# 1080 products with unread results behind the last needed one, in 60 patterns of operand addresses and widths

## The chip, the cores and the metric

The kernel runs on one core of a Trainium2 chip, as one launch. The core has a matrix engine (TensorE, PE in the profile, with its weight loads shown apart as PEld), three engines for elementwise work (VectorE or DVE, ScalarE or ACT, GpSimd or POOL), and SyncE (SP), which here only issues DMAs. TensorE multiplies a stationary operand of up to 128 x 128 numbers, which a weight load puts into the array, with a moving operand of up to 512 columns, and writes into PSUM, a memory of eight banks. The operands lie in SBUF, the on-chip memory of 128 partitions.

The metric is the device time of the launch in microseconds (us), lower is better.

## The reference

A two-layer encoder trunk over 256 frames and 16 learned meta tokens, width 2048. Layer 0 has gated linear attention (four heads) and stick-breaking attention (eight heads) behind one input projection and one output projection; layer 1 is a Mamba-2 mixer with eight groups. Each layer ends in a residual sum and a layer norm. In shortened form:

```python
h = concat([pad, meta, x], axis=1)
f = even_mixer(h, valid, ev_w_in, ..., ev_w_out)
h = layer_norm(ALPHA * h + f, ln_g[0], ln_b[0])
f = odd_mixer(h, valid, od_w_in, ..., od_w_out)
h = layer_norm(ALPHA * h + f, ln_g[1], ln_b[1])
return h[:, PREFIX:]
```

All arrays are float32. The output is 256 x 2048.

## The kernel before

The weights come from memory in units of 128 x 2048 numbers (1 MB each), one DMA per unit on SP's queue into the tile `raw`. Each half unit is split into a high part `whi` and a low part `wlo` (`split_into`, L144 to L146: ACT copies with rounding, DVE or POOL subtracts), both of type float32r, in which a product takes one pass of the array. The activations are split in the same manner into `xhi` and `xlo`, each of 16 blocks of 288 columns, of which a product reads up to 274. A full product is then three float32r products: high by high, high by low, low by high (`three`, L163 to L165). Two of the three use the same stationary tile `whi`, and the weight load stands ahead of each of them all the same.

An input unit (`in_unit`) is 16 blocks times three products, 48 in a row, into one PSUM tile `pj`. Its moving operand has 272 columns, or 260 where the unit is "C" (it starts at column 12 of a block) or 256 where it is "z" (it starts at column 16). A block starts 288 columns behind the one before. An output unit of layer 1 (`out1_half`, L421 to L423) turns it round: the activations `yh`, `yl` are stationary and 512 columns of the weights move. Between such rows of products stand the small products of the mixers, as steps of generators that `tick` takes in turn.

The order on each engine is fixed when the program is built, by a scheduler that goes by the recorded order and priorities. Each engine runs its own list, and semaphores join the lists.

The end of the program is `tail` (L1098 on). It splits the last four weight units; two of these go into `xhi` and `xlo`, which are free by then and seen there as flat rows (of 4608 columns; 4096 are written). Then come the last output products of two token halves of 128 rows each (the second half's last 512 columns in two pieces of 256), the sums into `acc` (L430), the statistics (L1133, L1137), the layer norm (L1139 to L1152) and five output DMAs (L1153, L1154). PSUM tiles named `po` come from two banks, those named `pj` from four. At the very end SP waits for all the output DMAs and for the last count of each engine, and then all engines meet twice (L1206 in the profile).

Of the kernel before, what the change touches and what calls it, by code (L numbers as in the profile page):

```python
# [12 lines left out]
P = 128  # L13
# [53 lines left out]
NU = len(L0) + len(L1)  # L67
# [20 lines left out]
class _Body:  # L88
# [1009 lines left out]
    def tail(self):  # L1098

        nc, lp = self.nc, self.lp  # L1100
        vec, pool = nc.vector, nc.gpsimd
        i0, g = NU - 4, NG - 1
        self.drain()
        self.load_unit(i0 + 2)
        for n, dq in enumerate((1, 2)):
            for h in range(2):
                src = self.raw[i0 + dq][:, h * 1024 : (h + 1) * 1024]
                o = slice((2 * n + h) * 1024, (2 * n + h + 1) * 1024)
                hi, lo = [a.rearrange("p k t -> p (k t)")[:, o] for a in (self.xhi, self.xlo)]
                nc.scalar.activation(hi, src, AF.Copy)  # L1110
                vec.tensor_tensor(lo, src, hi.bitcast(F32), op=ALU.subtract)
                self.parts[i0 + dq, h] = (hi, lo)
            if n == 0:
                self.load_unit(i0 + 3)
        lg = self.hp.tile([P, D], F32, tag="hacc", name="lg")
        lb = lp.tile([P, D], F32, tag="M", name="lb")
        nc.sync.dma_start(lg, self.lnr_d[0].partition_broadcast(P))
        nc.sync.dma_start(lb, self.lnr_d[1].partition_broadcast(P))
        for h in range(2):
            self.split_half(i0 + 3, h)  # L1120
        for t in range(2):
            st = lp.tile([P, 8, 6], F32, tag="fst", name=self.nm("fst"), bufs=2)
            acc = self.acc[:, t, :]
            for dq in range(4):
                halves = (0, 1) if t == 1 and dq == 3 else (None,)
                for b in halves:
                    ps = self.pj()
                    for h in range(2):
                        self.out1_half(ps, g, t, *self.parts[i0 + dq, h], h, b)
                    self.out1_add(ps, g, t, dq, b)  # L1130
                    with self.tc.high_priority():
                        for c in range(2) if b is None else (b,):
                            vec.bn_stats(st[:, 2 * dq + c, :], acc[:, dq * 512 + c * 256 : dq * 512 + (c + 1) * 256])  # L1133
            mv = lp.tile([P, 2], F32, tag="fmv", name=self.nm("fmv"), bufs=2)
            v, r, tm, mr = [lp.tile([P, 1], F32, tag=f"f{n}", name=self.nm("f"), bufs=2) for n in range(4)]
            with self.tc.high_priority():
                vec.bn_aggr(mv, st)  # L1137
                vec.tensor_scalar(v, mv[:, 1:2], LN_EPS, None, op0=ALU.add)
                nc.scalar.activation(r, v, AF.Ln)  # L1139
                nc.scalar.activation(r, r, AF.Exp, scale=-0.5)  # L1140
                self.newton(r, v, tm)
                vec.scalar_tensor_tensor(mr, mv[:, 0:1], -1.0, r, op0=ALU.mult, op1=ALU.mult)
            cut = (0, 1024, 2048) if t == 0 else (0, 384, 1216, 2048)
            ch = [slice(a, b) for a, b in zip(cut, cut[1:])]
            for cs in ch[1:]:
                vec.scalar_tensor_tensor(acc[:, cs], acc[:, cs], mv[:, 0:1], lg[:, cs], op0=ALU.subtract, op1=ALU.mult)  # L1146
            a = acc[:, ch[0]]
            nc.scalar.activation(a, a, AF.Identity, bias=mr, scale=r)  # L1148
            pool.tensor_tensor(a, a, lg[:, ch[0]], op=ALU.mult)  # L1149
            pool.tensor_tensor(a, a, lb[:, ch[0]], op=ALU.add)  # L1150
            for cs in ch[1:]:
                vec.scalar_tensor_tensor(acc[:, cs], acc[:, cs], r, lb[:, cs], op0=ALU.mult, op1=ALU.add)  # L1152
                nc.sync.dma_start(self.out[t * P : (t + 1) * P, cs], acc[:, cs])  # L1153
            nc.sync.dma_start(self.out[t * P : (t + 1) * P, ch[0]], a)  # L1154


def _pack(i):
# [53 lines left out]
```

## Time and profile before

| what | value |
|---|---|
| time, median of 2 runs | 1452.59 us (1452.31 to 1452.87) |
| the profiled execution's own time | 1453.08 us |
| its span, from the first to the last instruction | 1451.4 us |
| what lies outside of the span | 1453.08 - 1451.4 = 1.68 us |
| TensorE products in the profile | 10780 records |
| granted TensorE clock, mean | 0.996 |

A product's record is longer than the distance to the next one: products overlap in the array, so a record of 0.29 us stands every 0.126 us. What one more product costs is therefore not its record's length but the distance from one start to the next, and that is read from the first and the last row of a stretch without gaps and the number of products in it. A float32 product that isn't float32r takes two passes and leaves two records.

### The profile page before, as it was taken

Reading aid. Unit: us, or ns where it says so; the run is one execution under the profiler, and the core shown is the slowest. Engines: PE = TensorE matmul, PEld = TensorE weight load, DVE = VectorE, ACT = ScalarE, POOL = GpSimd, SP = SyncE. Lnnn points to the kernel's source line nnn. Section 1 sums busy time; section 2 is a strip of 40 time slices with the busy share of each in tenths; the row PEclk is TensorE's granted clock in tenths of the full one; section 3 lists DMA queues with packets and bytes.
Section 4 is the critical chain, followed back from the end, with each engine's and each line's share of the span. In section 5 each row is a group of like instructions: output and inputs, shape, how many; then the busy total and the mean of one; then the engine's idle time right before and its main releaser. Section 6 shows DMA issues by size and latency. Waiting matters only on the chain. (4 is left out here: it accounts for less than half of the span.)

```text
span 1451.4 us, 26046 instructions
## 1 busy us (share of the span) xinstructions
PE 1435.8 (99%) x10780; PEld 1360.0 (94%) x10780; DVE 985.9 (68%) x1516; ACT 761.9 (52%) x1125; POOL 346.3 (24%) x297
## 2 busy tenths in 40 slices
PE   9999999999999999999999999999999999999996
PEld 7999999999999999999999999899898998989975
DVE  8646575574564455446899979576876767768577
ACT  5535454454345444445577756555555555555541
POOL 4000000000101010112601435342432433434322
PEclk9999999999999999999999999999999999999998
DMA  7544444445444445434445554564554555444551
GB/s 259 203 163 161 158 156 157 170 146 175 147 173 149 142 145 175 164 141 146 145 146 213 193 205 164 203 222 169 198 175 167 199 180 215 153 171 171 203 204 58
DMA packets 36566, 249.82 MB, mean 172 GB/s; under 512 B 4128, under 2 KB 4960, under 8 KB 7776
## 3 DMA queue, kind: packets, MB, share of 16 engines
q1 hardware_dynamic: 36304, 247.90, 48.6%
q8 instruction: 84, 1.38, 0.4%
q14 instruction: 34, 0.28, 0.1%
q10 hardware_dynamic: 144, 0.26, 0.1%
HBM read 245.94 MB, written 2.20 MB: 171 GB/s over the span
## 5 line engine op out<-in xcount | busy, mean ns | idle before, releaser
L163 PE MATMUL pj<-xhi,whi 128*128 128x272 f32 (+4 forms) x2560 | 739.5, 289 | 1.9 <-ACT whi L145 1.6
L165 PE MATMUL pj<-xhi,wlo 128*128 128x272 f32 (+4 forms) x2560 | 737.7, 288 | 0.0
L164 PE MATMUL pj<-xlo,whi 128*128 128x272 f32 (+4 forms) x2560 | 734.6, 287 | 0.0
L146 DVE TENSOR_TENSOR wlo<-raw,whi 128x1024 fp32r<-128x1024 f32 (+1 forms) x402 | 512.0, 1276 | 293.2 <-ACT whi L145 292.1
L145 ACT ACTIVATE whi<-raw 128x1024 fp32r<-128x1024 f32 (+1 forms) x432 | 452.6, 1049 | 422.1 <-PE pj L164 349.7
L163 PEld LDWEIGHTS pj<-xhi,whi 128*128 128x128 f32 x2560 | 481.4, 188 | 5.7 <-ACT whi L145 2.3
L164 PEld LDWEIGHTS pj<-xlo,whi 128*128 128x128 f32 x2560 | 482.2, 188 | 1.7 <-DVE xlo L292 0.4
L165 PEld LDWEIGHTS pj<-xhi,wlo 128*128 128x128 f32 x2560 | 481.3, 188 | 2.3 <-DVE xlo L292 1.3
L163 PE MATMUL pj<-mixh,whi 128*128 128x272 f32 x384 | 112.4, 294 | 0.0
L164 PE MATMUL pj<-mixl,whi 128*128 128x272 f32 x384 | 111.1, 290 | 0.0
L165 PE MATMUL pj<-mixh,wlo 128*128 128x272 f32 x384 | 111.0, 289 | 0.0
L146 POOL TENSOR_TENSOR wlo<-raw,whi 128x1024 fp32r<-128x1024 f32 x30 | 73.8, 2461 | 140.7 <-ACT whi L145 140.7
L421 PE MATMUL pj<-whi,yh 128*128 128x512 f32 (+1 forms) x244 | 98.2, 402 | 0.0
L423 PE MATMUL pj<-whi,yl 128*128 128x512 f32 (+1 forms) x244 | 96.0, 393 | 0.0
L422 PE MATMUL pj<-wlo,yh 128*128 128x512 f32 (+1 forms) x244 | 95.6, 392 | 0.0
L252 POOL TENSOR_TENSOR gr<-gr,gsc 128x1088 f32<-128x1088 f32 x6 | 15.4, 2575 | 295.8 <-ACT gsc L251 295.8
L164 PEld LDWEIGHTS pj<-mixl,whi 128*128 128x128 f32 x384 | 72.3, 188 | 0.3
L163 PEld LDWEIGHTS pj<-mixh,whi 128*128 128x128 f32 x384 | 72.1, 188 | 0.5
L165 PEld LDWEIGHTS pj<-mixh,wlo 128*128 128x128 f32 x384 | 72.3, 188 | 0.1
L430 DVE SCALAR_TENSOR_TENSOR acc<-pj,rr,acc 128x512 f32<-128x512 f32 (+1 forms) x65 | 47.4, 737 | 30.3 <-PE pj L423 30.3
L1072 POOL TENSOR_TENSOR yu<-yu,gz 128x256 f32<-128x256 f32 x32 | 41.7, 1310 | 89.6 <-DVE yu L1071 89.4
L423 PEld LDWEIGHTS pj<-whi,yl 128*128 128x128 f32 x244 | 46.0, 188 | 10.6
(304 smaller groups left out, 1520.2 us busy)
## 6 DMA issues: line engine op xcount, KB each, us to landing
raw<-in_wts SPq DMA_DIRECT2D x214, 1024.0 KB, 4.8
ebc<-edr SPq DMA_DIRECT2D x8, 1664.0 KB, 6.7
hacc<-in_xT SPq DMA_DIRECT2D x8, 272.0 KB, 6.3
raw<-in_wts SPq DMA_DIRECT2D x8, 256.0 KB, 5.3
lg<-in_lnr SPq DMA_DIRECT2D x1, 1024.0 KB, 4.8
lb<-in_lnr SPq DMA_DIRECT2D x1, 1024.0 KB, 6.1
out_h<-acc SPq DMA_DIRECT2D x2, 512.0 KB, 2.6
out_h<-acc SPq DMA_DIRECT2D x2, 416.0 KB, 2.5
```

The costliest lines, as they stand in the source:

```text
L145: self.nc.scalar.activation(hi, src, AF.Copy)
L146: eng.tensor_tensor(lo, src, hi.bitcast(F32), op=ALU.subtract)
L163: mm(ps, whi, xhi, start=first, stop=False)
L164: mm(ps, whi, xlo, start=False, stop=False)
L165: mm(ps, wlo, xhi, start=False, stop=last)
L252: mul(c, c, e, op=ALU.mult)
L421: mm(ps, yh[:, kk, tt], hi[:, k, :], start=kk == 0, stop=False)
L422: mm(ps, yh[:, kk, tt], lo[:, k, :], start=False, stop=False)
L423: mm(ps, yl[:, kk, tt], hi[:, k, :], start=False, stop=kk == 3)
L430: self.nc.vector.scalar_tensor_tensor(a, ps, r[:, t : t + 1], a, op0=ALU.mult, op1=ALU.add)
L1072: nc.gpsimd.tensor_tensor(u, u, z[:, j, :], op=ALU.mult)
```

## The change

A new function `rest` is called at the end of `tail`. It adds 60 patterns; each takes a `po` tile and issues 6 rounds of three products of the same form as the needed ones (high by high, high by low, low by high), 18 in all, that add up in that tile. Nobody reads the tile. The moving operand is a piece of `xhi` or `xlo`, seen as a flat row, that begins at column `xo + k * pitch` in round k; the stationary operand is 128 columns of the last unit's first half (`whi`, `wlo`) that begin at `wo + k * 128`. A column is a float of 4 bytes. The patterns differ in the start `xo` (steps of 2, 4, 8 and 16 columns), in a start of `xlo` of its own, in the start `wo` of the weights (or of the low ones alone), in the order of the three products, in the pitch (320 by default; 336, 368, 384, 512) and in the number of columns (256 to 274, and 512). The default pitch of 320 columns and the weights' 128 keep every round of a pattern at the same place modulo 64 columns; in the needed products the step of 288 columns changes that place by 32 from block to block. The parameters `step`, `st`, `mv`, `back` and `rep` are left at their defaults in all 60 calls.

```diff
@@ tail
             nc.sync.dma_start(self.out[t * P : (t + 1) * P, ch[0]], a)
+        self.rest()
+
+    def rest(self):
+
+        mm = self.nc.tensor.matmul
+        xh, xl = [a.rearrange("p k t -> p (k t)") for a in (self.xhi, self.xlo)]
+        wh, wl = self.parts[NU - 1, 0]
+
+        def pattern(n, xo=0, xlo=None, wo=0, wlo=None, pitch=320, wp=P, m=P, step=1, order=0, st=None, mv=None, rep=6, back=False):
+            ps = self.po()
+            xlo = xo if xlo is None else xlo
+            wlo = wo if wlo is None else wlo
+            for k in range(rep):
+                a, b = st or (wh, wl)
+                if step == 1:
+                    hi, lo = [t[:, o + k * wp : o + k * wp + m] for t, o in ((a, wo), (b, wlo))]
...
+                c, d = mv or (xh, xl)
+                p, q = [t[:, o + k * pitch : o + k * pitch + n] for t, o in ((c, xo), (d, xlo))]
...
+                seq = [[(hi, p), (hi, q), (lo, p)], [(hi, q), (hi, p), (lo, p)], [(hi, p), (lo, p), (hi, q)]][order]
+                for i, (s, v) in enumerate(seq):
+                    self.nc.tensor.matmul(ps[:m, :n], s, v, start=k == 0 and i == 0, stop=k == rep - 1 and i == 2)
+
+        for o in (8, 24, 40, 56, 4, 12, 20, 28, 36, 44, 52, 60, 46, 50, 2, 62):
+            pattern(272, xo=o)
+        for o in (8, 16, 24, 32, 40, 48, 56):
+            pattern(272, xo=48, wo=o)
+        for o in (16, 32, 48):
+            pattern(272, xo=48, wo=0, wlo=o)
+        for o, p in ((48, 0), (48, 16), (48, 32), (32, 48), (0, 56), (0, 40)):
+            pattern(272, xo=o, xlo=p)
+        for o in (1, 2):
+            pattern(272, xo=48, order=o)
+        for o in (336, 384, 368):
+            pattern(272, xo=48, pitch=o)
+        for n, o in ((268, 0), (270, 0), (268, 48), (270, 48), (264, 48), (264, 32), (264, 16)):
+            pattern(n, xo=o)
+        for o in (40, 44, 52, 56):
+            pattern(256, xo=o)
+        for o in (16, 32, 48):
+            pattern(256, xo=48, wo=o)
+        for o in (44, 48, 12):
+            pattern(260, xo=o)
+        for o in (16, 32, 48):
+            pattern(512, pitch=512, wo=o)
+        for o in (8, 56):
+            pattern(512, pitch=512, xo=o)
+        pattern(274, xo=32)
```

Where the scheduler puts the new products is the first question. TensorE's list before ends with the last output products of `tail` (`pj` is the PSUM tile, `yh` and `yl` the stationary activations; the number is that of the buffer):

```order
L421 MATMUL pj_15657<-whi_15500,yh_15127 128x256 [waits DVE_49]
L422 MATMUL pj_15657<-wlo_15501,yh_15127 128x256
...
L421 MATMUL pj_15657<-whi_15504,yh_15127 128x256
L422 MATMUL pj_15657<-wlo_15505,yh_15127 128x256
L423 MATMUL pj_15657<-whi_15504,yl_15128 128x256
L1206 UNCONDITIONAL_BRANCH
```

TensorE's list after the change, at the beginning of the first pattern, the beginning of the second, and the end of the last:

```order
L422 MATMUL pj_15657<-wlo_15505,yh_15127 128x256
L423 MATMUL pj_15657<-whi_15504,yl_15128 128x256
L1179 MATMUL po_15695<-xhi,whi_15500 128x272 [waits PE_49]
L1179 MATMUL po_15695<-xlo,whi_15500 128x272
L1179 MATMUL po_15695<-xhi,wlo_15501 128x272
...
L1179 MATMUL po_15714<-xhi,whi_15500 128x272 [waits PE_49]
...
L1179 MATMUL po_16816<-xhi,wlo_15501 128x274
L1257 UNCONDITIONAL_BRANCH
```

All 1080 stand behind the last needed product, and nothing ahead of them has moved. The first product of each pattern waits for a count of TensorE itself (`PE_49`): that of the last product which wrote the same of the two `po` banks, from the third pattern on the pattern before the last.

SyncE's list ends with the output DMAs, before the change:

```order
L1154 DMA out_h<-acc 128x1024 [waits Pool_49]
L1153 DMA out_h<-acc 128x832 [waits DMAHW3_49,DVE_49]
L1153 DMA out_h<-acc 128x832 [waits DVE_49]
L1154 DMA out_h<-acc 128x384 [waits DMAHW5_49,Pool_49]
L1206 UNCONDITIONAL_BRANCH
```

and after it:

```order
L1154 DMA out_h<-acc 128x1024 [waits Pool_49]
L1153 DMA out_h<-acc 128x832 [waits DMAHW3_49,DVE_49]
L1153 DMA out_h<-acc 128x832 [waits DVE_49]
L1154 DMA out_h<-acc 128x384 [waits DMAHW5_49,Pool_49]
L1257 UNCONDITIONAL_BRANCH
```

Only the line number of the end has changed there, as on DVE, ACT and POOL: none of them waits for a new product until the end of the program.

More of the change, by code (lines that the diff above doesn't have):

```diff
@@ L1154, in tail @@
             nc.sync.dma_start(self.out[t * P : (t + 1) * P, ch[0]], a)
+        self.rest()
[11 more added lines that the diff above has]
+                    hi, lo = [t[:, o + k * wp : o + k * wp + m] for t, o in ((a, wo), (b, wlo))]
+                else:
+                    hi, lo = [t[:, o + k : o + k + step * (m - 1) + 1 : step] for t, o in ((a, wo), (b, wlo))]
+                c, d = mv or (xh, xl)
+                p, q = [t[:, o + k * pitch : o + k * pitch + n] for t, o in ((c, xo), (d, xlo))]
+                if back:
+                    p, q = p[:, ::-1], q[:, ::-1]
+                seq = [[(hi, p), (hi, q), (lo, p)], [(hi, q), (hi, p), (lo, p)], [(hi, p), (lo, p), (hi, q)]][order]
[26 more added lines that the diff above has]
+        pattern(274, xo=32)
```

## The prediction

> **What bounds the kernel now.** I read the page first, then busy time by windows at the end, then TensorE's rows in order of time in stretches without gaps, and last the groups of such a stretch, for the number of products in it. The page's head, its first two parts:
>
> ```profile
> span 1451.4 us, 26046 instructions
> PE 1435.8 (99%) x10780; PEld 1360.0 (94%) x10780; DVE 985.9 (68%) x1516; ACT 761.9 (52%) x1125; POOL 346.3 (24%) x297
> PE   9999999999999999999999999999999999999996
> PEclk9999999999999999999999999999999999999998
> ```
>
> TensorE is busy 1435.8 of 1451.4 us, so it idles 15.6 us in all, and the only slice of the 40 that isn't full is the last. Its clock is granted in full until then. Work added to TensorE can hide only in that idle time. Where it lies is told by the busy times of the end:
>
> ```profile
> core 0: us, PE busy (x) PEld busy (x) DVE busy (x) ACT busy (x) POOL busy (x), PEclk, DMA share, GB/s
> 1440.48:1451.40 10.92, 0.00 (x0) 0.00 (x0) 6.70 (x12) 1.11 (x3) 3.73 (x3) 0.59 0.36 144
> ```
>
> From 1440.48 us on TensorE does nothing for 10.92 us, while the other engines finish the layer norm and store it. That leaves 15.6 - 10.9 = 4.7 us of idle time for the rest of the span. The rows that frame the end, in order of time:
>
> ```profile
> 1440.19 0.28 PE L423 MATMUL pj<-whi,yl 128*128 128x256 f32 x1
> 1440.50 0.48 DVE L430 SCALAR_TENSOR_TENSOR acc<-pj,rr,acc 128x256 f32<-128x256 f32 x1 [0.42 <-PE pj L423]
> 1448.29 0.33 SPq L1154 DMA_DIRECT2D out_h<-acc  x1
> out_h<-acc SPq DMA_DIRECT2D x1, 192.0 KB, 2.1
> ```
>
> The last needed product starts at 1440.19. The last output DMA is issued at 1448.29 and takes 2.1 us to land, at 1450.4. The span ends at 1451.4: 1.0 us go by between the last thing that SyncE waits for and the end.
>
> **The change, part by part.** It removes and moves nothing. The needed work runs as before, in the same order and with the same waits, so the needed products still end where they did. It adds 60 patterns of 18 products, each with a weight load ahead of it, all behind the row at 1440.19. They use no DMA, and no other engine waits for them but SyncE at the very end, behind the output DMAs, for TensorE's last count. There is nothing queued behind them.
>
> What one of them costs is the distance between starts. For 272 columns, TensorE's rows in order of time, and the groups of the window 1320 to 1329.99:
>
> ```profile
> 1319.88 0.28 PE L164 MATMUL pj<-xlo,whi 128*128 128x272 f32 x1
> 1320.00 0.30 PE L165 MATMUL pj<-xhi,wlo 128*128 128x272 f32 x1
> 1320.14 0.29 PE L163 MATMUL pj<-xhi,whi 128*128 128x272 f32 x1
> ...
> 1329.97 0.29 PE L163 MATMUL pj<-xhi,whi 128*128 128x272 f32 x1
> ...
> L163 PE MATMUL pj<-xhi,whi 128*128 128x272 f32 x28 | 8.1, 288 | 0.0
> L165 PE MATMUL pj<-xhi,wlo 128*128 128x272 f32 x27 | 7.9, 292 | 0.0
> L164 PE MATMUL pj<-xlo,whi 128*128 128x272 f32 x27 | 7.7, 286 | 0.0
> ```
>
> The window holds 82 products, of which two (at 1319.76 and 1319.88) began before it. So 80 starts, 79 distances, lie from 1320.00 to 1329.97: 9.97 / 79 = 126.2 ns. As a unit is 48 products, the stretch holds a change of PSUM tile, and no idle time with it: the first product of a pattern costs no more than the others, if its wait is met. It is: the count it waits for is that of the pattern before the last, 18 products and over 2 us earlier. The distances aren't all equal: 0.12 us from 1319.88 to 1320.00, then 0.14 to 1320.14. For 256 columns:
>
> ```profile
> 1345.69 0.28 PE L164 MATMUL pj<-xlo,whi 128*128 128x256 f32 x1
> 1359.94 0.28 PE L165 MATMUL pj<-xhi,wlo 128*128 128x256 f32 x1
> L163 PE MATMUL pj<-xhi,whi 128*128 128x256 f32 x41 | 11.6, 283 | 0.0
> L165 PE MATMUL pj<-xhi,wlo 128*128 128x256 f32 x41 | 11.6, 282 | 0.0
> L164 PE MATMUL pj<-xlo,whi 128*128 128x256 f32 x41 | 11.5, 280 | 0.0
> ```
>
> 123 products, one of which began before the window: 121 distances in 14.25 us, 117.8 ns. For 512 columns, in the window 1388.1 to 1399.9:
>
> ```profile
> 1388.08 0.40 PE L422 MATMUL pj<-wlo,yh 128*128 128x512 f32 x1
> 1399.80 0.40 PE L421 MATMUL pj<-whi,yh 128*128 128x512 f32 x1
> L421 PE MATMUL pj<-whi,yh 128*128 128x512 f32 x18 | 7.1, 396 | 0.0
> L423 PE MATMUL pj<-whi,yl 128*128 128x512 f32 x17 | 6.7, 397 | 0.0
> L422 PE MATMUL pj<-wlo,yh 128*128 128x512 f32 x17 | 6.7, 397 | 0.0
> ```
>
> 52 products, two of which began before the window, the later at 1388.08: 50 distances in 11.72 us, 234.4 ns. For 260 columns, whose blocks begin at column 12, which is no multiple of 16:
>
> ```profile
> 1223.13 0.28 PE L163 MATMUL pj<-xhi,whi 128*128 128x260 f32 x1
> 1228.60 0.28 PE L164 MATMUL pj<-xlo,whi 128*128 128x260 f32 x1
> L164 PE MATMUL pj<-xlo,whi 128*128 128x260 f32 x16 | 4.5, 283 | 0.0
> L163 PE MATMUL pj<-xhi,whi 128*128 128x260 f32 x16 | 4.5, 280 | 0.0
> L165 PE MATMUL pj<-xhi,wlo 128*128 128x260 f32 x15 | 4.2, 282 | 0.0
> ```
>
> 47 products, 46 distances in 5.47 us: 118.9 ns. For the widths between, I go in a straight line from 260 to 272: 121.3 ns for 264, 123.8 for 268, 125.0 for 270; for 274, 126.2 x 274 / 272 = 127.1.
>
> The sum, with the number of patterns of each width from the diff (16 + 7 + 3 + 6 + 2 + 3 = 37 of 272 columns):
>
> - 272 columns: 37 x 18 = 666 products x 126.2 ns = 84.0 us
> - 268 and 270: 36 x 123.8 + 36 x 125.0 ns = 9.0 us
> - 264: 54 x 121.3 ns = 6.5 us
> - 256: 7 x 18 = 126 x 117.8 ns = 14.8 us
> - 260: 54 x 118.9 ns = 6.4 us
> - 512: 5 x 18 = 90 x 234.4 ns = 21.1 us
> - 274: 18 x 127.1 ns = 2.3 us
>
> Together 144.2 us of TensorE time. The first added product starts one distance behind the last needed one, at 1440.19 + 0.12 = 1440.31. The last one starts at 1440.31 + 144.2 - 0.13 = 1584.4; its record is 0.3 us long and ends at 1584.7. With the 1.0 us of the end the span is 1585.7 us. So of the 144.2 us some 10 run beside the layer norm and the output DMAs, and 134 stretch the span. The cover is the end of the program itself: the output has landed at 1450.4, when only a fourteenth of the products is done. The profiled execution took 1.68 us more than its span, which gives 1587.4, and it lay 0.49 us above the median, so against the median I predict 1587 us.
>
> What the trace doesn't show is the speed at the new starts: moving operands at 2, 4 or 8 columns off a multiple of 16, weights at 8 to 56 columns off, and rounds that all keep the same place modulo 64 columns. I bound it by the two distances above. The added products have 666 x 272 + 36 x 268 + 36 x 270 + 54 x 264 + 126 x 256 + 54 x 260 + 90 x 512 + 18 x 274 = 312,084 columns. At 0.12 us per 272 columns they take 137.7 us, at 0.14 us they take 160.6. That gives 1580 and 1603. I take the mean of the needed products, 144.2, since the 260-column row, at a start that is no multiple of 16, lies by the column (0.457 ns) between 256 (0.460) and 512 (0.458): in this one case such a start costs nothing.
>
> **The rivals.** First, patterns that stay at one place run faster than needed products whose blocks change it. For it speaks that distances in one stretch differ (0.12 and 0.14), so that a fixed place could hold the short one; against it that the mean by the column is the same within 2% at three widths and several starts. Below 0.12 per 272 columns the time is under 1580. The distance measured is 126.2 ns for 272 columns and 234.4 for 512. The Trainium skill, "TensorE: Matmul & The Clock Gate", section "Back-to-back issue gap", gives N / 2.4 + 2.5 ns for a warm array, 115.8 and 215.8 ns: this trace disagrees by 8 to 9%. By that rule the added products would take 312,084 / 2.4 ns + 1080 x 2.5 ns = 132.7 us, an estimate from that page, and the time would be about 1575 us.
>
> Second, a start off a multiple of 16 columns is dear. It is the moving start of the first 16 patterns, of four of 256, two of 260 and two of 512 columns. If each such product took twice its distance, that would add 16 x 18 x 126.2 + 72 x 117.8 + 36 x 118.9 + 36 x 234.4 ns = 57.5 us, 1644 us in all. From 28% of that price on (16 us) the time leaves my range. Against it speaks the 260-column row; for it, that no row shows a start off a multiple of 4.
>
> Third, on the other side: the products cost no time that can be told from none. That needs at most 10 us that hide at the end and 29 us (2% of 1452.59) besides, 39 us / 1080 = 36 ns per product, where the shortest width takes 117.8; or the unread products don't run at all. The built order has all 1080, on the one engine that is full.
>
> Fourth, the array's clock falls while nothing but products runs. At half the clock 144 us become 288, some 1731 us. The slices show full clock through 1440 us of the same load.
>
> **How the numbers follow.** The forecast, 1580 to 1603, gets 0.81; faster places 0.08; dear starts 0.09; hidden or not run 0.01; a lower clock 0.01. The range is that of the forecast, which leaves 0.19 outside. A time within 2% of 1452.59, about what a measurement of this kernel can tell from no change, comes from the third rival alone: 0.01. Faster has no case here. Slower gets 0.99.
>
> **What would show it.** In the profile after, all needed rows stand at the same times, the row at 1440.19 too; the first row of the new line follows 0.12 us later, and the last of it starts near 1584.4. The TensorE records rise by 1080. The last output DMA lands near 1450 as before, and the chain that ended last is TensorE's new line. The forecast is wrong if patterns differ by more than 0.12 to 0.14 us per 272 columns, if a gap stands at the first product of each pattern (60 of them at 0.3 us, a record's length, would be 18 us), or if the row at 1440.19 has moved.

## The result

The changed kernel takes 1585.7 us (two runs, 1585.48 and 1585.91) against 1452.59 before: a ratio of 1.0917, 95% interval 1.0897 to 1.0936. Predicted were 1587 us, range 1580 to 1603. The profiled execution took 1585.91 us with a span of 1584.3.

The head of the page of the changed kernel, and its slices for TensorE and DVE:

```profile
span 1584.3 us, 28206 instructions
PE 1579.1 (100%) x11860; PEld 1499.1 (95%) x11860; DVE 985.7 (62%) x1516; ACT 762.2 (48%) x1125; POOL 345.4 (22%) x297
PE   9999999999999999999999999999999999999999
...
DVE  8656565655644544588997968586777768574000
```

TensorE has 1080 records more, and its last slice is full now. DVE has the same number of instructions and, within 0.2 us, the same busy time as before, and does nothing in the last three slices. The busy times of the end, split where the last output DMA has landed (issued at 1447.62, 2.2 us to landing, so about 1449.9):

```profile
core 0: us, PE busy (x) PEld busy (x) DVE busy (x) ACT busy (x) POOL busy (x), PEclk, DMA share, GB/s
1439.58:1449.90 10.32, 10.32 (x85) 10.32 (x84) 6.72 (x12) 1.12 (x3) 3.97 (x3) 1.00 0.38 152
1449.90:1584.30 134.40, 133.41 (x999) 129.23 (x998) 0.00 (x0) 0.00 (x0) 0.00 (x0) 1.00 0.00 1
```

For 10.3 us the added products run beside the layer norm and the output; for the next 133.4 us they run alone, at the full granted clock, and 1.0 us is left for the end. The chain of waits that ended last has them as one piece without a gap, and TensorE's rows in order of time show where each width begins:

```profile
1439.74 143.57 PE po L1179 x1080
```

```profile
1439.46 0.28 PE L423 MATMUL pj<-whi,yl 128*128 128x256 f32 x1
1439.58 0.29 PE L1179 MATMUL po<-xhi,whi 128*128 128x272 f32 x1
...
1523.04 0.28 PE L1179 MATMUL po<-xhi,whi 128*128 128x268 f32 x1
...
1532.00 0.28 PE L1179 MATMUL po<-xhi,whi 128*128 128x264 f32 x1
...
1538.58 0.28 PE L1179 MATMUL po<-xhi,whi 128*128 128x256 f32 x1
...
1553.53 0.28 PE L1179 MATMUL po<-xhi,whi 128*128 128x260 f32 x1
...
1559.99 0.39 PE L1179 MATMUL po<-xhi,whi 128*128 128x512 f32 x1
...
1580.88 0.29 PE L1179 MATMUL po<-xhi,whi 128*128 128x274 f32 x1
...
1583.03 0.29 PE L1179 MATMUL po<-xhi,wlo 128*128 128x274 f32 x1
```

The difference of two such rows is what a width took, beside the term of the prediction (the 274-column term is 17 distances and one more of the same size):

| columns | products | predicted us | measured us | ns each |
|---|---|---|---|---|
| 272 | 666 | 84.0 | 83.46 | 125.3 |
| 268, 270 | 72 | 9.0 | 8.96 | 124.4 |
| 264 | 54 | 6.5 | 6.58 | 121.9 |
| 256 | 126 | 14.8 | 14.95 | 118.7 |
| 260 | 54 | 6.4 | 6.46 | 119.6 |
| 512 | 90 | 21.1 | 20.89 | 232.1 |
| 274 | 18 | 2.3 | 2.28 | 126.5 |
| all | 1080 | 144.2 | 143.6 | |

Read pattern by pattern in the same way, the 37 patterns of 272 columns lie between 123.3 and 127.3 ns. The four whose start is 2 columns off a multiple of 4 (46, 50, 2, 62) take 127.3, 126.3, 126.7 and 126.2.

### The profile page after: what moved, and what is told of

Same layout as the page of the kernel before. It is cut to its first block, busy times and chain, and to the rows that moved or that the text cites. A ratio compares the mean times of both kernels' runs of the same rounds, so it can differ in the third digit from the quotient of the medians.

```text
span 1584.3 us, 28206 instructions
## 1 busy us (share of the span) xinstructions
PE 1579.1 (100%) x11860; PEld 1499.1 (95%) x11860; DVE 985.7 (62%) x1516; ACT 762.2 (48%) x1125; POOL 345.4 (22%) x297
## 5 line engine op out<-in xcount | busy, mean ns | idle before, releaser
L1179 PE MATMUL po<-xhi,whi 128*128 128x272 f32 (+7 forms) x360 | 106.4, 296 | 0.0
L1179 PE MATMUL po<-xlo,whi 128*128 128x272 f32 (+7 forms) x360 | 106.4, 296 | 0.0
L1179 PE MATMUL po<-xhi,wlo 128*128 128x272 f32 (+7 forms) x360 | 106.3, 295 | 0.0
```

The lines of the kernel that those rows point to most:

```text
L1179: self.nc.tensor.matmul(ps[:m, :n], s, v, start=k == 0 and i == 0, stop=k == rep - 1 and i == 2)
```

## The experiments

**Half of the products.** The same patterns with three rounds.

```diff
-... order=0, st=None, mv=None, rep=6, back=False):
+... order=0, st=None, mv=None, rep=3, back=False):
```

> The same 60 patterns with 3 rounds of three products instead of 6: 540 products of the same widths and places, so half of the columns, and still 60 pattern starts. Theory (the cost is the distance from start to start times the number of products, a pattern's start costs nothing): the 143.5 us that the 1080 products took from the first start to the end become 71.7, the time 1585.7 - 71.7 = 1514.0 us. Rival (a pattern's start costs something of its own, say 0.2 us of the 143.5 us' 60 starts): the starts stay, only (143.5 - 12) / 2 = 66 us go, 1520 us.

Measured: 1514.26 us. From the start of the last needed product to that of the last added one, in TensorE's rows:

```profile
1440.09 0.28 PE L423 MATMUL pj<-whi,yl 128*128 128x256 f32 x1
...
1511.85 0.30 PE L1179 MATMUL po<-xhi,wlo 128*128 128x274 f32 x1
```

71.76 us for 540 products; in the changed kernel it is 1583.03 - 1439.46 = 143.57 for 1080. Both are 132.9 ns per product, with 60 pattern starts in each. A start costs nothing that shows.

**All patterns in one bank.** A second `po` tile is taken and dropped ahead of each pattern.

```diff
+            self.po()
             ps = self.po()
```

> All 60 patterns write the same one of the two po banks, so the first product of each waits for the count of the last product of the pattern right before it, which is not yet met when it could start. Theory (the waits of the changed kernel are free because they are met by then, and an unmet one costs the drain): each of 59 starts comes 0.17 us later (a record of 0.30 us against a distance of 0.126) or some more for the semaphore: 1585.7 + 10 to 15 = 1596 to 1601 us. Rival (a wait of TensorE for its own count never costs anything, as products run in order anyway): 1585.7 us.

Measured: 1585.95 us. This is the rival's number, but it decides nothing. In the built program each pattern from the third on still waits for the count of the pattern before the last: the tile that nothing writes has not changed the banks, so the waits stayed the same. The trace agrees: the first product of a pattern starts 132.8 ns behind the product ahead of it in the mean, any other one 133.0 ns. The question was put again, with single products, below.

**The products ahead of the last needed ones.** The call is moved from the end of `tail` to the place before its loop over the two token halves.

```diff
-        self.rest()
...
+        self.rest()
         for t in range(2):
```

> The same 1080 products stand ahead of the last output products of the tail, not behind them. Theory (some 10 us of the products ran beside the layer norm and the output DMAs, 133 stretched the span): now all of it stretches the span, 1452.6 + 143.5 = 1596 us, 10 us more than behind. Rival (nothing was hidden at the end, the sum was right by chance, or the end could hide as much ahead): 1585.7 us within 2.

Measured: 1595.58 us, 9.9 us more than with the products behind (9.6 more than the one-bank run, which has them behind too and was timed beside this one). The scheduler has mixed the added products with needed ones: between them stand some of the 512-column products of the tail, two at most places, and 39 needed products follow the last added one. All 1080 are ahead of these 39. The busy times of the end:

```profile
core 0: us, PE busy (x) PEld busy (x) DVE busy (x) ACT busy (x) POOL busy (x), PEclk, DMA share, GB/s
1583.70:1593.70 10.00, 0.00 (x0) 0.00 (x0) 5.79 (x10) 1.11 (x3) 2.68 (x2) 0.68 0.27 105
```

TensorE idles at the end again, and all of the added work stretches the span. The cover of 10 us is real, and it is the place that gives it.

**Distances by width, place, stationary columns and type.** 38 other patterns, the last three with operands cast to bfloat16.

```diff
+        for n in (256, 264, 272, 320, 384, 448, 512):
+            pattern(n, xo=48, pitch=512 if n > 300 else 320)
+        for o in (0, 8, 16, 24, 32, 40, 48, 56):
+            pattern(512, pitch=512, wo=o)
+        pattern(512, pitch=512, xo=48, wo=48)
+        for o in (24, 48, 48, 0, 48, 0, 0, 48):
+            pattern(272, xo=o)
+        for o in (0, 8, 16, 24, 32, 40, 56):
+            pattern(256, xo=o)
+        for m in (64, 32):
+            pattern(272, xo=48, m=m)
+            pattern(512, pitch=512, m=m)
+        for n in (256, 272, 512):
+            pattern(n, pitch=n if n > 300 else 320, st=sb, mv=mb)
```

> Another 38 patterns in place of the 60, read from the profile pattern by pattern (a cast of 4096 columns to bfloat16 on DVE besides, for the last three). Theory A (a float32r product takes 3.0 ns + 0.449 ns for each column at every width, places matter by 2 to 3%, and the extra over 1/2.4 ns a column comes from moving operands of 4 bytes): 256, 264, 272, 320, 384, 448, 512 columns at one place take 118, 121.5, 125, 147, 175, 204, 233 ns; stationary tiles of 64 or 32 columns change nothing; bfloat16 operands take 109, 116, 216 ns for 256, 272, 512 columns. Theory B (the extra comes from the weight loads that run beside the products): 64 and 32 stationary columns bring 272 columns near 116 ns and 512 near 216, bfloat16 does too as its loads are shorter. Places: 512 columns fall from 234 to 229 ns as the weights' start goes from 0 to 48 columns off a multiple of 64; 272 columns at place 48 take 123.4 ns whatever ran before (theory place), or 123.4 or 126.2 by what ran before (theory history). The time is about 1554 us by A.

Measured: 1552.86 us, in one execution. The first three products of the first pattern stand 17 us ahead of the rest, between needed products. TensorE's rows where the patterns named below begin, 18 distances from one row to the next where no dots stand between them, and at the end merged rows of products with bfloat16 operands:

```profile
1454.72 0.39 PE L1179 MATMUL po<-xhi,whi 128*128 128x512 f32 x1
1458.92 0.40 PE L1179 MATMUL po<-xhi,whi 128*128 128x512 f32 x1
1463.03 0.39 PE L1179 MATMUL po<-xhi,whi 128*128 128x512 f32 x1
...
1471.42 0.39 PE L1179 MATMUL po<-xhi,whi 128*128 128x512 f32 x1
1475.63 0.39 PE L1179 MATMUL po<-xhi,whi 128*128 128x512 f32 x1
...
1498.74 0.29 PE L1179 MATMUL po<-xhi,whi 128*128 128x272 f32 x1
1500.96 0.29 PE L1179 MATMUL po<-xhi,whi 128*128 128x272 f32 x1
1503.18 0.28 PE L1179 MATMUL po<-xhi,whi 128*128 128x272 f32 x1
...
1529.36 0.29 PE L1179 MATMUL po<-xhi,whi 128*64 128x272 f32 x1
1531.60 0.39 PE L1179 MATMUL po<-xhi,whi 128*64 128x512 f32 x1
1535.73 0.29 PE L1179 MATMUL po<-xhi,whi 128*32 128x272 f32 x1
...
1542.27 2.02 PE L1179 MATMUL po<-xb 128*128 128x256 bf16 x17
1544.24 2.02 PE L1179 MATMUL po<-xb 128*128 128x272 bf16 x16
1546.64 3.40 PE L1179 MATMUL po<-xb 128*128 128x512 bf16 x15
```

- Width, at place 48, over the last 12 distances of a pattern: 117.8, 120.0, 123.3, 146.5, 173.3, 202.2 and 233.3 ns for 256, 264, 272, 320, 384, 448 and 512 columns. The straight line 3.0 + 0.449 n of theory A meets them within 2%.
- Half the stationary columns: 272 columns take (1531.60 - 1529.36) / 18 = 124.4 ns, 512 take (1535.73 - 1531.60) / 18 = 229.4; a quarter takes 124.6 and 232.1. The weight loads did get shorter, some 134 and 109 ns for 64 and 32 columns against 187 ns for 128, and nothing falls to 116 or 216, so theory B, the weight loads, falls in this form.
- bfloat16: a merged row of n records is n - 1 distances and one record long. Without that record (0.27, 0.28 and 0.38 us) the three rows give 1.75 us for 16 distances, 1.74 for 15 and 3.02 for 14: 109, 116 and 216 ns for 256, 272 and 512 columns. So with two-byte operands the rule of the prediction's first rival (109.2, 115.8 and 215.8 ns) holds to the nanosecond, and float32r is what it misses here. Whether the moving or the stationary operand's four bytes do it stays open, since bfloat16 changes both.
- Places: 512 columns take (1463.03 - 1458.92) / 18 = 228.3 ns with the weights at place 0 (227.4 once the pattern has settled) and (1475.63 - 1471.42) / 18 = 233.9 at place 24. By 8 columns from 0 to 56: 227, 233, 233, 234, 232, 234, 229, 233 ns. The expectation had 234 at place 0, taken over from needed products whose stationary operand stands at place 24; it was wrong there. The moving operand's start acts as well: with the weights at place 0 and the moving operand at place 48, 512 columns take (1458.92 - 1454.72) / 18 = 233.3.
- History: 272 columns at place 48 take 123.3 ns from 1498.74 to 1500.96, behind a pattern at place 24 that takes 126.7, and again in the one behind it and at both later turns. The place decides, not what ran before.

**Single products that wait.** 180 patterns of one product each, between patterns of 18.

```diff
+        for g in range(180):
+            ps = self.po()
+            o = 48 + g % 6 * 320
+            self.nc.tensor.matmul(ps[:, :272], wh[:, :P], xh[:, o : o + 272], start=True, stop=True)
```

> Behind the needed products stand 10 patterns of 272 columns at place 48 (18 products each, waits met long before), then 180 patterns of one product each, same width and place, in turn on the two po banks, then 5 of the first kind again. Each single one waits for the count of the product two ahead of it, which ends only 0.30 us after its start. Theory (an unmet wait of TensorE for its own count holds the product back until the drain): two products per 0.30 us or more, so at least 150 ns each against 123.3 in the patterns of 18; 180 of them take 27 us or more. Rival (such a wait costs nothing at all): 123 to 126 ns each, 22.3 us.

Measured: 1516.4 us, in one execution. TensorE's last row ahead of the single products, the first four of them with the weight loads (PEld) of the third and the fourth, and the first row behind them:

```profile
1461.70 0.29 PE L1179 MATMUL po<-xhi,wlo 128*128 128x272 f32 x1
1461.82 0.28 PE L1186 MATMUL po<-xhi,whi 128*128 128x272 f32 x1
1462.05 0.39 PE L1186 MATMUL po<-xhi,whi 128*128 128x272 f32 x1
1462.16 0.19 PEld L1186 LDWEIGHTS po<-xhi,whi 128*128 128x128 f32 x1
1462.28 0.29 PE L1186 MATMUL po<-xhi,whi 128*128 128x272 f32 x1
1462.49 0.19 PEld L1186 LDWEIGHTS po<-xhi,whi 128*128 128x128 f32 x1
1462.50 0.40 PE L1186 MATMUL po<-xhi,whi 128*128 128x272 f32 x1
...
1502.53 0.29 PE L1179 MATMUL po<-xhi,whi 128*128 128x272 f32 x1
```

180 products take 1502.53 - 1461.82 = 40.7 us, 226 ns each, where the patterns of 18 on both sides take 123.3. In such a chain the unmet wait costs 103 ns per product. The direction was right, the size was not: the drain alone, 0.30 us per two products, gave 150. The rows show what it left out: the wait holds back the weight load too. In the patterns a load begins some 0.12 us ahead of its product and runs beside the product before it. Here it begins only 55 to 58 ns after the end of the product two ahead (1461.82 + 0.28 = 1462.10, load at 1462.16), in all 178 cases, and its product ends 396 ns after the load's begin, in the mean. As each product waits for the one two ahead, 57 + 396 = 453 ns go by for two products, which are the 226 ns each. Raising the count is not what costs: in the kernel before, the distance behind the 551 products in gapless rows of 272 columns that raise it is 126.3 ns in the mean, behind the others 125.9. And the met waits cost nothing: at place 48 a pattern of 18 with its start takes exactly 18 x 123.3.

**Places in the needed products.** Three kernels without the added products. The first begins the blocks of `xhi` and `xlo` 48 columns off a multiple of 64 and puts them 320 columns apart; the second takes 40 columns and also moves the stationary `yh`, `yl` to place 0; the third is the kernel before with only that last move. The first diff leaves out four constant tiles that are now made in layer 0; the second kernel has 40 and 24 where it shows 48 and 16.

```diff
-XW = 288
+XW, XO = 320, 48
...
-            self.xhi = cp.tile([P, KT, XW], F32R, tag="xhi", name="xhi")
-            self.xlo = cp.tile([P, KT, XW], F32R, tag="xlo", name="xlo")
+            self.xhi, self.xlo = [
+                cp.tile([P, KT * XW + o], F32R, tag=n, name=n)[:, o:].rearrange("p (k t) -> p k t", t=XW)
+                for n, o in (("xhi", XO), ("xlo", 0))
+            ]
+            cp.tile([P, 16], F32, tag="pad", name="pad")
```

```diff
+        lp.tile([P, 40], F32, tag="ypad", name="ypad")
         self.acc = lp.tile([P, 2, D], F32, tag="acc", name="acc")
```

> The kernel before, without the added products, with the activations' blocks 320 columns apart and begun 48 columns off a multiple of 64 (four constant tiles move to a pool of layer 0 to make room). Place theory (272 columns at place 48 take 123.3 ns and at the mix of places before 125.9; 256 columns at place 0 take 120.0, before 117.4): 5856 x -2.6 ns + 1488 x +2.6 ns + 336 x +0.5 ns = -11 us, 1441 us. Rival (the distances in the needed rows are set by their surroundings, not by the place): 1452 us within 2.

> As the run before, with the blocks begun 40 columns off, so that the 256-column pieces begin at place 56, and with the stationary activations of the output units of layer 1 moved from place 24 to place 0. Place theory: 5568 x (123.5 - 125.9) ns + 1488 x (118.3 - 117.4) ns + 756 x (227.4 - 234.3) ns = -13.4 + 1.3 - 5.2 = -17 us, 1435 us. Rival (surroundings, not places): 1452 us within 2.

> The kernel before, without the added products, with a pad of 40 columns that moves the stationary activations of layer 1's output units from place 24 to place 0 and nothing else of TensorE's operands there. Place theory: 756 products of 512 columns x (227.4 - 234.3) ns = -5.2 us, 1447 us. Rival (the place of the stationary tile acts only in the unread patterns, where rounds repeat one place): 1452 us within 1.

| kernel | us | ratio to before, 95% interval | expected |
|---|---|---|---|
| place 48 | 1443.55 | 0.9935, 0.9922 to 0.9949 | 1441 |
| place 40 and `yh` at 0 | 1439.64 | 0.9908, 0.9893 to 0.9923 | 1435 |
| `yh` at 0 alone | 1448.39 | 0.9969, 0.9958 to 0.9981 | 1447 |

They were timed against 1452.26 us for the kernel before on the same chip. All three gains are under 1%, and each interval excludes no gain. Rows of the first, a stretch of 272 columns and the groups of the window 1308.01 to 1318:

```profile
1308.03 0.29 PE L163 MATMUL pj<-xhi,whi 128*128 128x272 f32 x1
...
1317.89 0.29 PE L165 MATMUL pj<-xhi,wlo 128*128 128x272 f32 x1
...
L163 PE MATMUL pj<-xhi,whi 128*128 128x272 f32 x27 | 7.7, 287 | 0.0
L165 PE MATMUL pj<-xhi,wlo 128*128 128x272 f32 x27 | 7.7, 287 | 0.0
L164 PE MATMUL pj<-xlo,whi 128*128 128x272 f32 x27 | 7.7, 287 | 0.0
```

81 products of 272 columns, 80 distances in 9.86 us: 123.3 ns, the unread pattern's number, against 126.2 in the prediction's stretch. Rows of the third, a stretch of 512 columns:

```profile
1383.12 0.39 PE L422 MATMUL pj<-wlo,yh 128*128 128x512 f32 x1
...
1394.91 0.39 PE L423 MATMUL pj<-whi,yl 128*128 128x512 f32 x1
...
L423 PE MATMUL pj<-whi,yl 128*128 128x512 f32 x19 | 7.4, 389 | 0.0
L421 PE MATMUL pj<-whi,yh 128*128 128x512 f32 x18 | 7.0, 389 | 0.0
L422 PE MATMUL pj<-wlo,yh 128*128 128x512 f32 x18 | 7.0, 389 | 0.0
```

The window 1383 to 1395 has 55 products, two of which began before it: 52 distances in 11.79 us, 226.7 ns, against 234.4. So places act in needed work as in unread work, and the rival of surroundings falls. Products whose place did not change did not change either: those of 272 columns on `mixh` and `mixl` take 126.0 ns in the first kernel as before. All three gains are some 75% of the forecast (8.7 of 11 us, 12.6 of 17, 3.9 of 5.2). In the third kernel the settled value was too low: the 700 distances between neighbouring 512-column products with nothing between them average 228.6 ns over the whole trace, not 227.4, against 234.1 before; 700 x 5.6 ns = 3.9 us are the whole gain, although the pad also moves the operands of layer 1's small products. In the first kernel the input products did reach their values, 123.4 ns at 272 columns and 119.8 at 256, and the profiled spans differ by 10.2 us; why the medians differ by 8.7 only stays open. The second kernel is the fastest of all here, 0.9% below the kernel before.

## Why the prediction was right

- *The place in the program.* All 1080 products run behind the last needed one, no other engine has changed, and the row 1439.58 follows the last needed product 0.12 us later, as said. The run with the products ahead shows that the place was worth 9.6 to 9.9 us, where the prediction had some 10.
- *The distance as the price.* Records are 0.28 to 0.40 us long; what counts is the distance, and half the products cost half the time to 0.1%. The sum was 144.2 us and came out at 143.6. No width is off by more than 1.1%. The terms that were too high by the most are 272 and 512 columns (0.5 and 0.2 us). That the sum came so close is in part luck of the mix: the prediction took the mean of needed products because the trace had no price for the new places, and single patterns of 272 columns lie up to 2.3% below it. Had all 37 stood at the fastest place, their term would have been 666 x 123.3 ns = 82.1 us, still within the range.
- *The waits at the pattern starts.* Predicted as free because they are met. Both halves are shown: met ones cost nothing that shows, and in a chain of unmet ones each product costs 103 ns more.
- *The end.* Last record's end 1583.03 + 0.29 = 1583.3, span 1584.3: the 1.0 us of the end holds. The time outside of the span is 1585.91 - 1584.3 = 1.6 us.
- *What is left of the difference.* The first added product starts 0.7 us sooner than in the profile of before, because the needed work ended sooner by that. Taken by its words, one of the prediction's signs of being wrong is met here, a moved row at 1440.19. It says little, since the added products come behind that row and the runs of the kernel before scatter by more (1451.37 to 1455.06 us over the runs beside the experiments). With the sum's 0.6 us that makes the 1.3 us between 1587 and 1585.7.
- *The rivals.* Faster places exist, 123.3 ns and 227 ns, but the mean over the patterns is 125.3 and 232.1: the first rival's mechanism is right for some places only and too small. Dear starts don't exist down to 2 columns, with at most 127.3 ns (the rival's list left out the two patterns whose `xlo` alone starts at 56 or 40 columns, 12 products that take 1.5 us in all). Hidden or dropped products and a lower clock are refuted by the windows above. The Trainium skill's rule ("TensorE: Matmul & The Clock Gate", "Back-to-back issue gap") is right for bfloat16 here and 7 to 8% low for these products (125.3 against 115.8, 232.1 against 215.8 ns), so the measured distances were the ones to go by.

## What to carry to other kernels

Price a product on a busy TensorE by the distance between starts of the same width and type in the trace, not by its record and not by a formula for another type; then subtract only what fits beside work that outlasts TensorE. The time that an engine idles at the end is a cover of fixed length, some 10 us here: work put there is free up to that length, and the same work ahead of the last needed products costs in full. When TensorE is the bound in float32r, try the start columns of its operands modulo 64: a pad of 40 columns was worth 0.3% here, and with a new start and pitch of the moving operands 0.9%.

## What was not expected

The start of an operand modulo 64 columns sets a float32r product's distance, reproducibly and by some 3%: 123.3 to 127.3 ns at 272 columns, 227 to 234 at 512, where the stationary operand's start alone is enough. Why a place is fast or slow stays open. With bfloat16 operands the distances are 109, 116 and 216 ns. And a product that waits for a count of its own engine that is not yet there pays more than the drain of the product ahead, 226 ns instead of 123, since its weight load waits as well and no longer runs beside another product.
